# The first down projection of a feed-forward layer: its instruction order written out on all engines

## The chip, the cores and the metric

The kernel runs on one core of one Trainium2 chip. The core has five engines, each with its own stream of instructions: TensorE (PE in the profile; its weight loads are PEld) multiplies 128x128 stationary tiles with 128x512 moving tiles; VectorE (DVE) does elementwise work and reads the accumulators; ScalarE (ACT) copies, squares and scales; GpSimd (POOL) does elementwise work between tiles in the on-chip memory; SyncE (SP) only issues transfers, and its stream is called the load queue here.

The metric is the device time of one execution, in microseconds (us).

## The reference

One layer of a diffusion backbone for 2048 tokens of width 1024 in float32: attention and a gated recurrence, an output projection, and then a gated feed-forward layer. What the change touches is the last part:

```python
def swiglu(h, w_gu, w_down):
    a, b = jnp.split(h @ w_gu, 2, axis=-1)
    return (jax.nn.silu(a) * b) @ w_down
...
        x = x + mx[5] * swiglu(modulate(rmsnorm(x, g_norm2[l]), mx[3], mx[4]), w_gu[l], w_down[l])
...
    return rmsnorm(x, g_final)
```

`w_gu` is 1024 x 5632 and `w_down` 2816 x 1024. The kernel keeps float32 accuracy by splitting each factor into a rounded high part and the rest (two tiles, "parts"), and multiplies high by high, high by low and low by high.

## The kernel before, in words

Attention, recurrence and output projection end at about 2010 us. The feed-forward layer then runs in four stages, and the tokens are handled as two pairs of 512-token blocks, pair 1 first: `hidden(1)`, `down(1)`, `hidden(0)`, `down(0)` (lines 1520 to 1526).

Both matrix products use a seven-product scheme (Strassen and Winograd's) over a 2x2 split: left factors A11, A12, A22 and sums S1 to S4, right factors B11, B21, B22 and sums T1 to T4. So there are seven products of half the size, and their accumulators are partly carried from one product to the next.

**`hidden(pair, side, made)`** (line 1243), the up projection, runs over 22 blocks of 128 columns. For each, `weights` loads two 512 KB pieces of `w_gu` into the pool `wraw` (two tiles of each of two tags), makes parts of A11 and A12, then the sums S1, S2, S4, S3 on GpSimd (`total`, pool `wsum`) and their parts (line 1264 copies on ScalarE, line 1265 subtracts). Line 1291 is its matmul, 12 per product. The results go to memory, with sums of them for the next stage (lines 1355 to 1361, stored at 1306). `made` is a generator that makes the right factors' parts during the first block; `side` is called after every second block. In pair 1 `side` is `right_sums` (line 1368): for each of 11 row blocks of `w_down` it loads four quadrants of 256 KB into the 10-tile pool `tmp`, makes four sums on VectorE (lines 1378 to 1384) and stores them.

**`down(pair, side)`** (line 1388), the down projection, has 7 products of 11 steps, so 77 steps. `load(i)` (lines 1415, 1416) fetches two 256 KB tiles into `wraw`; `exact(i)` makes their parts, two copies on ScalarE (line 1429) and two subtractions on VectorE (line 1430); `mms(i, t)` (line 1484) does 3 matmuls for each of 4 token blocks, 12 in a step. In pair 1 the parts lie in two sets of tiles, `dwa` and `dwb`, for even and odd steps; in pair 0 they lie in the 32 tiles of `vA`. After the last step of a product `emptied` (line 1453) handles one of its four accumulators in each following step: gate product on VectorE (line 1460), addition to the row block on GpSimd (line 1461), for the fourth to sixth product a square on ScalarE (line 1446), for the fifth another product on GpSimd (line 1466), and for the sixth the row's normalization: sum (1450) and mean (119) on VectorE, a power on GpSimd (121), scaling on VectorE (1469) and the store (1470). The last product does the same at the end (1474, 1476, 1477). `side` is called in every sixth step; in pair 1 it is `build(0)` (line 1201), which reloads the other pair's right factors (line 1214) and makes their parts (lines 1112, 1113) and sums (1177, 1206, 1228), several tiles in one call.

**Order.** A planner arranges each engine's stream from the program's order, priorities and its own estimate of times; it may take instructions of one stage ahead of another's. `tc.high_priority()` moves a piece forward. `tc.manual_schedule(engines=...)` marks a region in which the named engines issue the region's instructions in the order of the program's text; where instructions from outside the region fall among them stays the planner's choice. Before, no such region lies in the feed-forward stages.

**Places.** The pools of `hidden` (`wva`, `wsum`, `wvb`) and those of `down` (`y0p`, `dwa`, `dwb`, `y1p`) share memory: `wva` lies where `y0p` lies, `wsum` where `dwa` lies, `wvb` where `dwb` and `y1p` lie. `vA` (32 tiles) and `vB` (24 tiles) hold the right factors' parts.

## Time and profile before

| | |
|---|---|
| median of 3 runs | 3375.32 us (3370.61 to 3377.19) |
| the profiled execution's own time | 3374.67 us |
| its span, first to last instruction | 3372.9 us |
| mean granted TensorE clock | 0.986 of full speed |
| busy share of the span: TensorE, VectorE, ScalarE, GpSimd | 96%, 54%, 47%, 53% |
| `hidden(1)` | about 2012 to 2465 us |
| `down(1)` | about 2465 to 2712 us |
| `hidden(0)` | about 2712 to 3148 us |
| `down(0)` and the end | 3148 to 3373 us |

How to read it: the profile's windows give, for a stretch of time, each engine's busy time and its count of instructions. TensorE's matmuls overlap, so its busy time nearly fills any stretch in which it is fed; a stretch's loss is better seen from its length against the count of its matmuls. The timeline's rows give start, length, engine, line, operation, output <- inputs with shape, count, and in brackets the idle time of the engine before the row and what ended it. Tile names are without their buffer numbers: `dh` and `dl` are the high and low parts of a down step in pair 1, `lr` the loaded tile, `pd1A` an accumulator, `y` a row block, `yg` the gate product, `sq` the square, `s` and `r` results of the up projection, `w` a loaded piece of `w_gu`, `wq` one of `w_down`; `x` stands for several tiles, the factors' parts among them.

### The profile page before, as it was taken

The page shows a single profiled execution, that of the slowest core. Times are in us where ns is not written, and L with a number is a line of the kernel's source. Part 1 is how long each engine was busy: PE and PEld are TensorE (multiplying, and loading weights), DVE is VectorE, ACT ScalarE, POOL GpSimd, SP SyncE. Part 2 cuts the span into 40 slices and gives each one's busy share as a digit, 9 for nine tenths or more (in the row PEclk, how much of TensorE's full clock was granted, in tenths as well). Part 3 has the DMA queues.
Part 4 walks back from the last instruction along what each step waited for, and adds up shares of the span by engine and source line. Part 5 has one row for each costly group of instructions (what it writes and reads, how often), then busy time and mean ns, then how long its engine had stood idle before and what let it go on. Part 6 is the DMA issues. An engine that isn't in the chain of part 4 may idle for free. (4 is left out here: it accounts for less than half of the span.)

```text
span 3372.9 us, 54914 instructions
## 1 busy us (share of the span) xinstructions
PE 3233.4 (96%) x20220; PEld 2682.1 (80%) x20220; DVE 1836.1 (54%) x3270; ACT 1597.1 (47%) x3327; POOL 1781.8 (53%) x1648
## 2 busy tenths in 40 slices
PE   8999999989999999999999999999979989999998
PEld 5998987987778778778787877888868778888887
DVE  6344555226666666666664556444366753333566
ACT  4322222237777777777764224333344443333444
POOL 4322223118788888888743117767631267666222
PEclk9999999989999999999999999999989999999999
DMA  7244565441111112111015343444565533323764
GB/s 240 87 150 128 164 180 159 121 118 38 42 31 51 56 51 77 38 39 58 18 30 181 119 140 120 159 160 162 170 236 185 191 120 107 97 95 109 252 198 162
DMA packets 358622, 408.04 MB, mean 121 GB/s; under 512 B 31856, under 2 KB 249936, under 8 KB 358096
## 3 DMA queue, kind: packets, MB, share of 16 engines
q1 hardware_dynamic: 358352, 404.53, 37.8%
q8 instruction: 159, 2.61, 0.3%
q14 instruction: 111, 0.91, 0.1%
HBM read 274.92 MB, written 129.52 MB: 120 GB/s over the span
## 5 line engine op out<-in xcount | busy, mean ns | idle before, releaser
L930 DVE TENSOR_REDUCE neg<-s 128x1 f32<-128x768 f32 x384 | 366.5, 955 | 217.3 <-PE s L927 215.9
L943 POOL TENSOR_TENSOR pr<-pr,lf 128x768 f32<-128x768 f32 x256 | 370.9, 1472 | 116.2 <-ACT lf L939 116.1
L927 PE MATMUL s<-K,qs 128*128 128x512 f32 (+1 forms) x1536 | 373.2, 366 | 38.5 <-ACT pr L935 37.1
L935 ACT ACTIVATE pr<-s,neg 128x768 f32<-128x768 f32 x384 | 349.5, 910 | 62.6 <-DVE neg L930 36.3
L927 PEld LDWEIGHTS s<-K,qs 128*128 128x128 f32 x1536 | 263.8, 192 | 118.9 <-ACT pr L935 58.8
L951 PE MATMUL pt<-identr,pr 128*128 128x128 f32 x2304 | 331.9, 277 | 16.8 <-ACT pf L957 12.8
L957 ACT ACTIVATE pf<-pt 128x512 f32<-128x512 f32 x448 | 259.6, 604 | 79.8 <-PE pt L951 76.9
L951 PEld LDWEIGHTS pt<-identr,pr 128*128 128x128 f32 x2304 | 263.6, 142 | 32.2 <-ACT pf L957 24.6
L965 PE MATMUL av<-pf,V 128*64 128x256 f32 x2304 | 260.0, 379 | 0.7 <-DVE neg L934 0.4
L1461 POOL TENSOR_TENSOR y<-y,yg 128x512 f32<-128x512 f32 x48 | 75.8, 1595 | 286.1 <-DVE yg L1460 282.3
L965 PEld LDWEIGHTS av<-pf,V 128*64 128x64 f32 x2304 | 161.3, 137 | 74.6 <-DVE Sb L740 0.6
L1430 DVE TENSOR_TENSOR x<-lr,x 128x512 fp32r<-128x512 f32 x154 | 119.8, 813 | 67.6 <-ACT x L1429 64.9
L1430 DVE TENSOR_TENSOR dl<-lr,dh 128x512 fp32r<-128x512 f32 x154 | 119.0, 810 | 66.3 <-ACT dh L1429 66.2
L1429 ACT ACTIVATE dh<-lr 128x512 fp32r<-128x512 f32 x154 | 89.5, 623 | 110.9 <-PE pd1A L1484 53.9
L1429 ACT ACTIVATE x<-lr 128x512 fp32r<-128x512 f32 x154 | 90.6, 626 | 93.7 <-PE pd0A L1484 38.5
L343 PE MATMUL f<-hTh,wh 128*128 128x512 f32 (+1 forms) x320 | 121.6, 380 | 6.7 <-ACT ft L372 6.7
L1291 PE MATMUL pA<-x,A11h 128*128 128x512 f32 x352 | 114.3, 405 | 8.3 <-ACT A11h L1264 6.0
L1484 PE MATMUL pd0A<-x,x 128*128 128x512 f32 x528 | 120.7, 389 | 0.0
L343 PE MATMUL f<-hTh,wl 128*128 128x512 f32 (+1 forms) x320 | 120.0, 375 | 0.0
L343 PE MATMUL f<-hTl,wh 128*128 128x512 f32 (+1 forms) x320 | 119.5, 373 | 0.0
L121 POOL TENSOR_TENSOR rs_qq<-ms_qq,mhalf 128x4 f32<-128x4 f32 x32 | 35.2, 1102 | 155.3 <-DVE ms_qq L119 151.2
L121 POOL TENSOR_TENSOR rs_x<-ms_x,mhalf 128x1 f32<-128x1 f32 x34 | 20.5, 605 | 181.5 <-DVE ms_x L119 181.5
(332 smaller groups left out, 9131.0 us busy)
## 6 DMA issues: line engine op xcount, KB each, us to landing
w<-in_w_gu_dram SPq DMA_DIRECT2D x88, 512.0 KB
wm<-in_w_mod_dram SPq DMA_DIRECT2D x24, 1024.0 KB
lr<-s_wT SPq DMA_DIRECT2D x88, 256.0 KB
lr<-in_w_down_dram SPq DMA_DIRECT2D x66, 256.0 KB
s_q<-sq SPq DMA_DIRECT2D x128, 128.0 KB
qs<-s_q SPq DMA_DIRECT2D x32, 512.0 KB
wq<-in_w_down_dram SPq DMA_DIRECT2D x44, 256.0 KB
s_wT<-wq SPq DMA_DIRECT2D x44, 256.0 KB
```

What stands on the lines that cost most here:

```text
L343: nc.tensor.matmul(pm[:, :n], w[wi][:, k, c0:c0 + P], hT[b][hi][:, k, :], start=(k == 0 and i == 0), stop=(k == KT - 1 and i == 2))
L927: nc.tensor.matmul(s[:, o:o + w], self.qs[:, hh, self.item[2], half, :], self.kv[0][:, k0 + o:k0 + o + w], start=(half == 0), stop=(half = ...
L930: nc.vector.tensor_reduce(neg[:, i:i + 1], s[:, :n], axis=AX.X, op=ALU.min)
L935: nc.scalar.activation(pr[:, k0:k0 + n], s[:, :n], AF.Exp, bias=neg[:, m:m + 1], scale=-1.0, accum_out=self.lf[:, hh, i, :1] if i < NSEG - ...
L943: nc.gpsimd.tensor_tensor(pj, pj, self.lf[:, hh, j, 1:].to_broadcast([P, SW]), op=ALU.mult)
L951: nc.tensor.transpose(pt[:, (2 * i + hh) * P:(2 * i + hh + 1) * P], self.prs[hh][:, (2 * k2 + i) * P:(2 * k2 + i + 1) * P], ident)
L957: nc.scalar.activation(pf, pt, AF.Copy)
L965: nc.tensor.matmul(self.av[i * 64:(i + 1) * 64], self.kv[1][:, 2 * k2 + i, :], self.pf[k2][:, i * 256:(i + 1) * 256], start=(n == 0), stop ...
L1291: nc.tensor.matmul(acc, w[wi][:, k, :], x[xi][k], start=(start and k == 0 and i == 0), stop=(stop and k == KH - 1 and i == 2), skip_group_ ...
L1429: nc.scalar.activation(hi, src, AF.Copy)
L1430: nc.vector.tensor_tensor(lo, src, f32v(hi), op=ALU.subtract)
L1484: nc.tensor.matmul(cur[t], l[:, t * P:(t + 1) * P], r, start=(start and j == 0 and f == 0), stop=(stop and j == NHF - 1 and f == 2), skip_ ...
```

## The change

1. `build` yields after every tile instead of after every group. `by_factor` restores the old grouping where it runs beside `hidden(1)`. In `down(1)` one tile's work is called in every step from step 8 on (it was a group in every sixth step).
2. `down(1)` is a `manual_schedule` region for all five engines, from after its first loads and parts to its end. `down(0)` is left to the planner.
3. `load` runs 4 steps ahead (it was 3), `exact` 2 steps ahead (it was 1), in pair 1 only up to step 35 and 1 from there on. Four loads and two steps' parts are made under high priority.
4. In pair 1 the parts of steps 0 to 7 lie in `vA`, those of steps 8 to 37 in `vB`, and in `dwa` and `dwb` from step 38 on.
5. The row blocks of pair 1 are loaded in steps 1, 3, 5, 7, 12, 14, 16, 18 (they were in 2 to 9). The stores of finished rows come two steps after their scaling.
6. The last product's work on a row block (`last`) is cut in three pieces: gate product, addition and square; sum, mean and power; scaling and store. The first piece of a token block comes ahead of the second of the one before it, and so on.
7. In the first block of `hidden(0)` S1 and S2 are made under high priority, S1's and S2's sums in `tmp` and their parts in `wva`.
8. `right_sums` is called after each of the first 11 blocks of `hidden(1)`.

The instructions are the same in number and kind. The diff, cut:

```diff
+            eng = nc.gpsimd if pair else nc.vector
...
                         nc.sync.dma_start(x, s_h2[tb][:, k, :])
-                    yield
+                        yield
...
+        def by_factor(steps):
+
+            for x in steps:
+                if x:
+                    yield
...
+                    soon = pair == 0 and ff == 0
...
-                        hi, lo = ((wva if n in ("A11", "A12") else wvb).tile([P, H, P], F32R, tag="v", name=f"{n}{x}{nm}")
+                        hi, lo = ((wva if n in ("A11", "A12") or soon and n in ("S1", "S2") else wvb).tile([P, H, P], F32R, tag="v", name=f"{n}{x}{nm}")
...
                     parts("S2", s2, nc.vector)
+                    if soon:
+                        yield out
...
                     nxt = first(order[0])
+                    if pair == 0:
+                        next(nxt[0])
...
                         h = {}
+                    if n < NHF:
                         next(side, 0)
...
-                        hi, lo = (slot(vA) if pair == 0 else
+                        hi, lo = (slot(vA) if pair == 0 or i < 8 else slot(vB) if i < 38 else
...
-                    (nc.vector if last else nc.gpsimd).tensor_tensor(y[:, cs], y[:, cs], x, op=ALU.add)
+                    nc.gpsimd.tensor_tensor(y[:, cs], y[:, cs], x, op=ALU.add)
...
-                        nc.sync.dma_start(out[0, row(0, t), :], y)
...
+                        stores.append((i + 2, tb, t))
+
+                def last(acc, t):
+
+                    y = ys[1, t]
+                    x = t512(f"yg{pair}l{t}")
+                    nc.vector.tensor_tensor(x, acc, gate2[:, :512], op=ALU.mult)
+                    nc.vector.tensor_tensor(y[:, :512], y[:, :512], x, op=ALU.add)
+                    square(1, 0, t)
+                    yield
+                    rs = norm(1, t)
+                    yield
+                    nc.vector.scalar_tensor_tensor(y[:, :512], y[:, :512], rs, gfin[:, :512],
+                                                   op0=ALU.mult, op1=ALU.mult)
+                    nc.scalar.activation(y[:, 512:], y[:, 512:], AF.Copy, scale=rs)
+                    nc.sync.dma_start(out[0, row(1, t), :], y)
+                    yield
...
+                stores = []
                 with tc.high_priority():
-                    for i in range(3):
+                    for i in range(4):
                         load(i)
                     exact(0)
+                    exact(1)
+                made = 2
...
+                written = ExitStack()
+                if pair:
+                    E = mybir.EngineType
+                    written.enter_context(tc.manual_schedule(engines={E.PE, E.DVE, E.Activation, E.Pool, E.SP}))
                 for i, (n, j) in enumerate(steps):
...
-                    load(i + 3)
-                    exact(i + 1)
+                    load(i + 4)
+                    ahead = 2 if pair == 0 or i < 36 else 1
+                    while made <= i + ahead:
+                        exact(made)
+                        made += 1
                     if i == 0:
                         nc.sync.dma_start(gate2, rows_bcast(modrow[0, 5 * D:6 * D]))
-                    if 2 <= i < 10:
-                        rows((i - 2) // 4, (i - 2) % 4)
+                    if i in ROWS[pair]:
+                        rows(*divmod(ROWS[pair].index(i), 4))
...
                     if pending:
                         emptied(*pending.pop(0))
+                    while stores and stores[0][0] <= i:
+                        _, tb, t = stores.pop(0)
+                        nc.sync.dma_start(out[0, row(tb, t), :], ys[tb, t])
...
-                    if i >= 4 and i % 6 == 0:
+                    if i >= 8:
                         next(side, 0)
+                under = []
                 for t in range(4):
                     for i in range(len(steps) - kept, len(steps)):
                         mms(i, t)
-                    emptied(len(plan) - 1, cur[t], t)
-
-        hidden(1, right_sums(), build(1))
+                    under.append(last(cur[t], t))
+                    for g in reversed(under):
+                        next(g, 0)
+                for _ in range(2):
+                    for g in reversed(under):
+                        next(g, 0)
+                written.close()
+
+        ROWS = (2, 3, 4, 5, 6, 7, 8, 9), (1, 3, 5, 7, 12, 14, 16, 18)
+        hidden(1, right_sums(), by_factor(build(1)))
```

More of the change, by code (lines that the diff above doesn't have):

```diff
@@ L1218, in build @@
                         parts(n, raw[r, 0, k], nc.vector, vA, vA)
-                    yield
-                for _ in early_sums():
-                    yield
+                        yield
+                for (r, tb), (r0, tb0), (r1, tb1) in EARLY:
+                    for k in range(KH):
+                        nc.vector.tensor_tensor(raw[r, tb, k], raw[r0, tb0, k], raw[r1, tb1, k], op=ALU.subtract)
+                        yield
             T1 = [raw.pop((0, 0, k)) for k in range(KH)]
             for t in T1:
-                parts("T1", t, nc.gpsimd if pair else nc.vector, vB, vB)
-            yield
+                parts("T1", t, eng, vB, vB)
+                yield
+            yield "T1"
             T2 = T1
@@ L1228, in build @@
                 nc.vector.tensor_tensor(t, raw[1, 1, k], t, op=ALU.subtract)
+                yield
             for t in T2:
                 parts("T2", t, nc.vector, vB, vB)
-            yield
+                yield
+            yield "T2"
             for k in range(KH):
-                parts("B22", raw.pop((1, 1, k)), nc.gpsimd if pair else nc.vector, vB, vB)
-            yield
-            T4 = [diff(raw.pop((1, 0, k)), T2.pop(0)) for k in range(KH)]
+                parts("B22", raw.pop((1, 1, k)), eng, vB, vB)
+                yield
+            yield "B22"
+            T4 = []
+            for k in range(KH):
+                T4.append(diff(raw.pop((1, 0, k)), T2.pop(0)))
+                yield
             for k in range(KH):
                 parts("T3", raw.pop((0, 1, k)), nc.vector, vA, vA)
-            yield
+                yield
+            yield "T3"
             for t in T4:
-                parts("T4", t, nc.gpsimd if pair else nc.vector, vA, vA)
-            yield
+                parts("T4", t, eng, vA, vA)
+                yield
+            yield "T4"
+        def by_factor(steps):
+            for x in steps:
+                if x:
+                    yield
         def hidden(pair, side, made):
@@ L1268, in total @@
                     def total(n, x, y, op):
-                        t = wsum.tile([P, H, P], F32, tag="s", name=f"{n}{nm}")
+                        t = t512(f"{n}{nm}").rearrange("p (h c) -> p h c", c=P) if soon and n in ("S1", "S2") else \
+                            wsum.tile([P, H, P], F32, tag="s", name=f"{n}{nm}")
                         nc.gpsimd.tensor_tensor(t, x, y, op=op)
```

14 lines of the change are left out of this document (5 added, 9 removed).

## The prediction

> **What bounds the kernel now.** I read the windows by stage first, then TensorE's timeline wherever a window is worse than its pace, then the other engines and the load queue (SP) at those places. The two feed-forward halves are limited by TensorE: from 2760 to 3148 us, and in the second pair's down projection after that, it never idles. The first pair's down projection (about 2465 to 2712) is the exception, and the change rewrites it. The first fence holds windows (length; busy time and count of each engine; clock; DMA share; GB/s), then the matmuls of line 1484 alone, then one TensorE row.
>
> ```profile
> 2451.00:2520.00 69.00, 52.17 (x200) 40.16 (x198) 48.56 (x71) 29.53 (x52) 23.02 (x9) 0.85 0.66 226
> 2520.00:2600.00 80.00, 77.64 (x340) 63.61 (x341) 48.95 (x67) 32.31 (x56) 13.42 (x9) 1.00 0.59 189
> 2600.00:2660.00 60.00, 55.89 (x242) 44.84 (x241) 44.67 (x55) 30.70 (x60) 17.72 (x12) 1.00 0.52 170
> 2660.00:2713.00 53.00, 50.47 (x209) 39.53 (x207) 34.02 (x53) 22.13 (x42) 10.27 (x9) 0.97 0.63 208
> 2713.00:2760.00 47.00, 39.27 (x153) 31.12 (x154) 28.93 (x40) 22.39 (x43) 32.21 (x26) 0.89 0.32 101
> 2760.00:3148.00 388.00, 388.00 (x1658) 311.93 (x1657) 138.06 (x160) 141.11 (x237) 260.70 (x195) 1.00 0.34 111
> ```
>
> ```profile
> 2451.00:2713.00 262.00, 221.69 (x924) 176.58 (x924) 0.95 0.60 198
> 3148.00:3364.00 216.00, 209.89 (x924) 173.43 (x924) 1.00 0.61 205
> ```
>
> ```profile
> 3359.82 4.24 PE L1484 MATMUL pd0A<-x,x 128*128 128x512 f32 x18
> ```
>
> The same 924 matmuls take 262 us here and 216 there (some matmuls of a neighbouring stage lie in each window). Eighteen in a row take 4.24 us, and the last is 0.39 us long, so the pace is (4.24 - 0.39) / 17 = 0.2265 us; a step of 12 is 2.72 us. In the up projection it is 388 / 1658 = 0.234 us. Length minus count times pace gives what each stretch loses: 69 - 45.3 = 23.7; 80 - 77.0 = 3.0; 60 - 54.8 = 5.2; 53 - 47.3 = 5.7; and 47 - 153 x 0.234 = 11.2 at the start of the next up projection. That is 48.8 us, all a change here can win.
>
> The start, in rows of a timeline (start, length, engine, line, what; in brackets the idle time before it and what ended it):
>
> ```profile
> 2476.23 0.79 PE L1484 MATMUL pd1A<-dl,dh 128*128 128x512 f32 x1 [1.54 <-DVE dl L1430]
> 2476.82 0.63 PE L1484 MATMUL pd1A<-dh,dl 128*128 128x512 f32 x1
> ...
> 2495.35 0.80 PE L1484 MATMUL pd1A<-dl,dh 128*128 128x512 f32 x1 [8.88 <-DVE dl L1430]
> ```
>
> ```profile
> 2472.70 12.47 POOL L1361 TENSOR_TENSOR s<-r,s 128x512 f32<-128x512 f32 x1 [6.10 <-DVE r L1348]
> 2485.20 0.33 SPq L1306 DMA_DIRECT2D s_hid1S<-s  x1
> 2491.26 0.63 ACT L1429 ACTIVATE dh<-lr 128x512 fp32r<-128x512 f32 x1 [5.87 <-DMA lr<-s_hid1A]
> ```
>
> The 8.88 us gap is a chain: VectorE is full of the other pair's factors, one GpSimd subtraction takes 12.47 us, its store heads the load queue until 2485.20, with the next step's load behind it, and ScalarE waits 5.87 us for that load. After gaps of 1.5 and 8.9 us the next matmuls are 0.63 us long instead of 0.39, so a gap costs some 1.5 us more.
>
> **The change part by part.** *Start of the stage.* Steps 0 to 7 put their parts in tiles of the old factors, two steps are prepared and four loaded under high priority, the other pair's factors come one tile per step from step 8 on, and the w_down sums are over by then. Every item of the chain above is gone. What is late next is one accumulator bank that waits for the last product of the old stage; nine matmuls (2 us) cover it. I leave 1.0 of the 23.7: **-22.7** (bounds -16.3, if stores still head the queue for the 5.87 us of the ScalarE row and the clock falls, and -23.7). DMA: a step needs 0.5 MB, from step 8 to 23 another 0.26 MB of factors, and between 12 and 18 also half a row block, so 1.05 MB in 2.72 us, 385 GB/s. This row gives 40 slices of the time from 2440 to 2712, and shows 401 reached:
>
> ```profile
> GB/s 380 401 342 236 352 89 71 290 283 170 222 89 237 217 173 217 96 235 200 182 143 216 180 219 176 170 192 232 171 198 128 134 137 175 224 177 220 325 254 112
> ```
>
> With four loads ahead I count nothing for it; without the lead, each GB/s short is a later load.
>
> *Two steps ahead up to step 35.* The 3.0 us of 2520 to 2600 are the emptied banks of the first products, where four additions on GpSimd (5.95 us) stretch four subtractions on VectorE to 5.46. A step ahead covers this: **-3.0** (bounds 0 and -3.0).
>
> ```profile
> 2515.58 5.95 POOL L1461 TENSOR_TENSOR y<-y,yg 128x512 f32<-128x512 f32 x4 [30.41 <-DVE yg L1460]
> 2517.21 5.46 DVE L1430 TENSOR_TENSOR dl<-lr,dh 128x512 fp32r<-128x512 f32 x4
> ```
>
> *The written order from step 36 on.* Here only one step is prepared ahead, in two sets of tiles, and the text puts the emptying of a bank between one step's parts and the next: gate product (VectorE), addition (GpSimd), square (ScalarE), for the sixth product also sum, mean, power and scaling of the row. In written order the square stands before the next step's copies on ScalarE. In the profile the planner did it the other way:
>
> ```profile
> 2637.35 1.29 DVE L1430 TENSOR_TENSOR dl<-lr,dh 128x512 fp32r<-128x512 f32 x2 [1.43 <-ACT dh L1429]
> 2638.56 0.68 DVE L1460 TENSOR_TENSOR yg<-pd1A,gate 128x512 f32<-128x512 f32 x1
> 2639.32 1.30 POOL L1461 TENSOR_TENSOR y<-y,yg 128x512 f32<-128x512 f32 x1 [19.40 <-DVE yg L1460]
> 2639.40 1.15 ACT L1429 ACTIVATE dh<-lr 128x512 fp32r<-128x512 f32 x2 [1.56 <-PE pd1A L1484]
> 2640.66 0.63 ACT L1446 ACTIVATE sq<-y 128x512 f32<-128x512 f32 x1
> ```
>
> ```profile
> 2617.37 0.63 ACT L1446 ACTIVATE sq<-y 128x512 f32<-128x512 f32 x1 [1.53 <-POOL y L1461]
> 2618.00 1.13 ACT L1429 ACTIVATE dh<-lr 128x512 fp32r<-128x512 f32 x2
> 2618.65 2.42 DVE L1430 TENSOR_TENSOR dl<-lr,dh 128x512 fp32r<-128x512 f32 x2 [0.16 <-ACT dh L1429]
> ```
>
> The copies (2639.40) ran while GpSimd added, the square after them (2640.66). In the new order one round is: copy to subtraction 0.65 (2618.00 to 2618.65), two subtractions 1.21 (2637.35 to 2638.56), gate product until the addition starts 0.76, addition 1.30 and 0.04 to the square, square until the next copy 0.63: 4.6 us against 2.72. Four banks are emptied: the last subtraction is done 4 x 4.6 + 0.65 + 1.29 = 20.3 us after the first copy, and TensorE, unhindered, would want it at 5 x 2.72 + 0.23 = 13.8. That is 6.5, and 1.5 for the slow matmuls behind the gap: **+8.0** for the fourth product. For the fifth, three of the four rounds also hold a copy (0.53) and a subtraction (0.60, half the pair's) of a factor: 3 x 5.7, and 5.1 for the last, whose subtractions meet the extra GpSimd product: 22.2 + 1.94 - 13.8 = 10.3, with the clock **+11.8**. For the sixth, VectorE itself waits in the middle:
>
> ```profile
> 2716.92 0.19 ACT L1446 ACTIVATION_READ_ACCUMULATOR sq<-y 128x1 f32 x1
> 2717.14 0.16 DVE L1450 TENSOR_TENSOR ss1f<-ssf 128x1 f32<-128x1 f32 x1 [0.19 <-ACT sq L1446]
> 2717.82 0.15 DVE L119 TENSOR_SCALAR ms_xf<-ss1f 128x1 f32<-128x1 f32 x1
> 2718.05 0.55 POOL L121 TENSOR_TENSOR rs_xf<-ms_xf,mhalf 128x1 f32<-128x1 f32 x1 [2.85 <-DVE ms_xf L119]
> 2690.57 1.28 DVE L1469 SCALAR_TENSOR_TENSOR y<-y,rs_xf,gfin 128x1024 f32<-128x1024 f32 x1 [0.38 <-POOL rs_xf L121]
> 2691.77 0.68 DVE L1430 TENSOR_TENSOR dl<-lr,dh 128x512 fp32r<-128x512 f32 x1
> ```
>
> From a copy to the square 3.96, square and its sum 0.73, then 0.03, sum 0.18, mean to power 0.23, power 0.55, 0.03, scaling 1.20 (2690.57 to 2691.77): 6.9. Subtraction to subtraction that is 6.9 - 0.65 = 6.26, and 6.86 in the three rounds that also hold a factor: 26.8 + 1.94 - 13.8 = 14.9, with the clock **+16.6**. The sum of the three is +36.4. The 5.2 + 5.7 lost there now fall away: **-10.9**. Bounds of the pair of terms: +15 (no slow matmuls, each round 0.5 us shorter) to +34 (each round 0.7 longer).
>
> The Trainium skill, Perfetto Trace Analysis, "Tensor Engine Instruction", calls ScalarE, VectorE and GpSimd strict first-in first-out, which is the rule that speaks against this part: what waits at the head holds all behind it. The trace agrees: the copy at 2618.00 starts as the square ends, and the square had waited 1.53 us.
>
> *Start of the next up projection.* S1 and S2 of its first block are made ahead, with places of their own. Now:
>
> ```profile
> 2728.15 1.22 PE L1291 MATMUL pA<-x,A11h 128*128 128x512 f32 x2 [6.01 <-ACT A11h L1264]
> 2729.14 0.61 ACT L1264 ACTIVATE S1h<-S 128x512 fp32r<-128x512 f32 x1
> 2697.28 11.07 SPq L1256 DMA_DIRECT2D w<-in_w_gu_dram  x4
> 2722.26 0.36 SPq L1477 DMA_DIRECT2D out_dram<-y  x1
> 2704.79 0.64 ACT L1264 ACTIVATE A11h<-w 128x512 fp32r<-128x512 f32 x1 [2.89 <-DMA w<-in_w_gu_dram]
> ```
>
> TensorE waits 6.01 us with the next block's product, and S1's copy runs only at 2729.14; had it been there, four products of 12 (11.2 us) would cover the rest. The first bank is free in time too: the gate product comes first in the new last piece. I leave 2 of 11.2: **-9.2** (bounds 0 and -11.2).
>
> *First sums moved.* The w_down sums run beside the first 11 blocks of the first up projection instead of every second one: the same 44 loads, 44 sums, 44 stores, now also at its start, where VectorE is busy 18.51 of 20 us:
>
> ```profile
> 2040.00:2060.00 20.00, 17.03 (x73) 13.08 (x71) 18.51 (x19) 13.00 (x24) 14.98 (x10) 0.99 0.00 1
> ```
>
> Four sums more are 4 x 0.60 = 2.4 us there. They are emitted behind the block's own work, so I take **+1.5** (bounds -1 and +6; the upper one is four loads short of a tile, waiting 1.5 us each). *Last tiles.* In the second pair the last square comes ahead of a scaled copy that waits: **-1**. Loads and two steps ahead in that pair: 0, as TensorE never idles there.
>
> Sum: -22.7 - 3.0 + 36.4 - 10.9 - 9.2 + 1.5 - 1 = **-8.9 us**. The profiled execution took 3374.67, 0.65 below the median; 3374.67 - 8.9 = 3365.8, so 3366. From no change a measurement tells 0.2%, 6.7 us, on either side.
>
> **The rivals.** (1) *Slower: the next weights queue behind the last stores.* Their loads are outside the written part. Should SP hold them behind the stores of the last finished rows, which wait for their scaling, they go out when the first store did, at 2722.26, 9 us after the down projection's end at 2713, and land 7.5 us later (2697.28 to 2704.79, the time until the first could be copied). TensorE then idles 16.5 us and has slow matmuls for 1.5 behind that, not 2 in all: +16.0 on the sum, 3382. From 15.6 us of added loss on (8.9 + 6.7) the change is slower by what can be told. For: a store at the head held the loads until 2485.20. Against: the four went out at 2697.28, well before the stores. (2) *The emptying is covered* after all, as the planner's order covered it (2.4 us of stretched subtractions, no TensorE gap at 2617): no +36, time 3330, and between this and the sum for half of it, 3348. Against: two sets of tiles and the order of the text. (3) *The first sums collide*: the ten other blocks each lose 1 to 2 us to a load that waits for one of the pool's 10 tiles (ten of 1 in place of the 1.5: 3374, of 2: 3384). Against: with a set in every second block TensorE was busy for 369.41 of 371 us there, by the window:
>
> ```profile
> 2080.00:2451.00 371.00, 369.41 (x1578) 296.66 (x1577) 160.45 (x190) 133.22 (x226) 256.26 (x187) 1.00 0.51 168
> ```
>
> (4) *No slow matmuls behind short gaps.* In this kernel that would take 1.5 from each of the three terms: 3361. The Trainium skill, TensorE: Matmul & The Clock Gate, "What's actually happening", has the clock fall only after an idle window of about 3.4 us. The trace does not bear that out here: the matmul at 2476.82 is 0.63 us long after a gap of 1.54.
>
> **How the numbers follow.** Forecast 0.48 (its own range 3357 to 3374), rival 1 0.18, rival 2 0.14, rival 3 0.12, rival 4 0.05, unnamed 0.03. Faster: 0.28 of the forecast, 0.14 of rival 2, 0.05 of rival 4: 0.47. Same: 0.20 of the forecast, 0.07 of rival 3, 0.03 of rival 1: 0.30. Slower: 0.15 of rival 1, 0.05 of rival 3 and the unnamed: 0.23. The range 3344 to 3388 leaves out the better half of rival 2 and the far end of rival 1.
>
> **What would show it.** Right: no gap over 2 us from the down projection's first matmul until the fourth product's banks are emptied; then three groups of four gaps, about 2, 3 and 4 us, each ended by the subtraction, with ScalarE's square waiting for GpSimd ahead of the copies, and VectorE's mean and scaling ahead of subtractions; S1's copy before the last down matmul. Wrong: a stage near 216 us (rival 2), a gap over 6 us ended by a w_gu load (rival 1), or gaps between 2100 and 2300 us (rival 3).

## The result and the profile after

The changed kernel took **3387.71 us** (median of 8 runs, 3381.48 to 3398.99), the kernel before, run beside it, 3372.49 us (8 runs, 3367.30 to 3377.19). The ratio is 1.0047, with a 95% interval of 1.0031 to 1.0063: slower by 0.47%, where 8.9 us, 0.26%, faster was forecast. The time lies within the range that the prediction gave (3344 to 3388), but at its far end and on the other side of no change. The profiled execution took 3384.43 us, its span is 3382.7 us, the clock 0.988.

The first views show where to look: up to TensorE's first up-projection matmul the program is unchanged, so time is counted from there.

```profile
L1291 PE MATMUL pA<-x,A11h x2: 394/396/397, 2011.9 to 2012.2; 128*128 128x512 f32 x2
```

```profile
L1317 PE MATMUL pA<-x,A11h x8: 392/397/400, 2006.0 to 2010.3; 128*128 128x512 f32 x8
```

The first row is of the kernel before, the second of the changed one: that line's TensorE instructions with their first and last start. To the span's end it is 3372.9 - 2011.9 = 1361.0 us before and 3382.7 - 2006.0 = 1376.7 after, **+15.7 us**. That is the medians' difference, 15.2; the spans differ by only 9.8 because this execution happened to come to the up projection 5.9 us sooner. It was 6.0 us ahead already at the last matmul of line 705 (1725.0 us against 1731.0), long before anything that the change touches.

The windows of the changed kernel (columns as in the prediction: length; busy time and count of TensorE, its weight loads, VectorE, ScalarE, GpSimd; clock; DMA share; GB/s):

```profile
2085.00:2461.00 376.00, 366.10 (x1545) 292.37 (x1544) 170.86 (x192) 132.57 (x227) 252.48 (x184) 0.99 0.50 163
2461.00:2510.00 49.00, 44.69 (x188) 35.99 (x187) 23.88 (x29) 18.05 (x30) 9.80 (x6) 0.97 0.67 236
2510.00:2595.00 85.00, 85.00 (x377) 70.35 (x376) 64.10 (x89) 38.23 (x66) 16.78 (x10) 1.00 0.67 229
2595.00:2633.00 38.00, 33.91 (x135) 25.70 (x134) 22.26 (x37) 17.63 (x35) 5.81 (x4) 0.96 0.48 153
2633.00:2674.00 41.00, 33.75 (x134) 25.66 (x134) 25.28 (x37) 18.14 (x36) 10.24 (x8) 0.96 0.43 141
2674.00:2713.00 39.00, 28.39 (x96) 20.88 (x95) 21.84 (x38) 14.15 (x29) 7.33 (x8) 0.82 0.49 162
2713.00:2760.00 47.00, 41.45 (x164) 31.95 (x163) 33.93 (x41) 22.57 (x44) 31.64 (x23) 0.93 0.36 119
```

With the prediction's paces (0.2265 us for a down matmul, 0.234 for an up matmul), length minus count times pace gives each stretch's loss:

| stretch | before | after | difference | predicted |
|---|---|---|---|---|
| first sums (2085 to 2461) | 1.7 | 14.5 | **+12.8** | +1.5 |
| start of `down(1)` (2461 to 2510) | 23.7 | 6.4 | **-17.3** | -22.7 |
| two steps ahead (2510 to 2595) | 3.0 | 0 | -3.0 | -3.0 |
| emptying of the 4th, 5th, 6th product (2595 to 2713) | 10.9 | 7.4 + 10.6 + 17.3 = 35.3 | +24.4 | +36.4 - 10.9 = +25.5 |
| start of `hidden(0)` (2713 to 2760) | 11.2 | 8.6 | **-2.6** | -9.2 |
| last tiles | 8.8 | 8.8 | 0 | -1 |
| sum | | | +14.3 | -8.9 |

The last row is the time from the end of the last matmul to the span's end. The 1.4 us between 14.3 and 15.7 lie outside these windows or in their edges.

*The first sums.* TensorE and ScalarE, then VectorE, then the load queue, all of the changed kernel. Line 1404 loads a quadrant of `w_down`, lines 1407 to 1413 are its sums, 1365 and 1358 a sum of the up projection and the copy that follows it, 1332 a store of its results:

```profile
2097.05 0.73 PE L1317 MATMUL pB<-x,S4h 128*128 128x512 f32 x2 [3.11 <-ACT r L1358]
2096.41 0.60 ACT L1358 ACTIVATE r<-pB 128x512 f32<-128x512 f32 x1 [5.59 <-DVE r L1365]
```

```profile
2088.33 0.69 DVE L1407 TENSOR_TENSOR wq<-wq,wq 128x512 f32<-128x512 f32 x1 [3.59 <-DMA wq<-in_w_down_dram]
...
2094.44 0.68 DVE L1407 TENSOR_TENSOR wq<-wq,wq 128x512 f32<-128x512 f32 x1
2095.04 0.68 DVE L1365 TENSOR_TENSOR r<-pB,r 128x512 f32<-128x512 f32 x1
```

```profile
2084.22 0.32 SPq L1332 DMA_DIRECT2D s_hid1S<-s  x1
2084.59 1.87 SPq L1404 DMA_DIRECT2D wq<-in_w_down_dram  x4
```

VectorE stands 3.59 us at a `w_down` sum whose load went out at 2084.59, behind a store. Five sums, the last of them of the next set, come ahead of the up projection's own sum at 2095.04; ScalarE's copy (line 1358) follows it, and TensorE has idled 3.11 us. Four more gaps of over 0.2 us follow, of 2.64, 2.04, 0.50 and 1.46 us, the last at 2258.85. Up to 2260 us all eleven sets of sums have begun (line 1407, from 2053.8 to 2256.2); in the kernel before it was five (line 1378, from 2093.6 to 2240.5).

*The emptying.* ScalarE and VectorE around the sixth product's rounds:

```profile
2685.20 0.63 ACT L1475 ACTIVATE sq<-y 128x512 f32<-128x512 f32 x1 [4.57 <-POOL y L1489]
...
2685.83 1.13 ACT L1458 ACTIVATE dh<-lr 128x512 fp32r<-128x512 f32 x2
```

```profile
2675.05 1.29 DVE L1459 TENSOR_TENSOR dl<-lr,dh 128x512 fp32r<-128x512 f32 x2 [0.82 <-ACT dh L1458]
...
2681.91 1.29 DVE L1459 TENSOR_TENSOR dl<-lr,dh 128x512 fp32r<-128x512 f32 x2
...
2688.17 1.29 DVE L1459 TENSOR_TENSOR dl<-lr,dh 128x512 fp32r<-128x512 f32 x2
```

The step's copies (2685.83) stand behind a square that waited 4.57 us for GpSimd. From subtraction to subtraction it is 6.86 and 6.26 us, the two values that the prediction gave for a round with and without a factor's tile.

*The start of `hidden(0)`.* TensorE, ScalarE and GpSimd:

```profile
2732.80 1.22 PE L1317 MATMUL pB<-x,S1h 128*128 128x512 f32 x2 [3.07 <-ACT S1h L1287]
```

```profile
2732.13 0.62 ACT L1287 ACTIVATE S1h<-S 128x512 fp32r<-128x512 f32 x1
```

```profile
2727.64 0.92 POOL L121 TENSOR_TENSOR rs_xf<-ms_xf,mhalf 128x1 f32<-128x1 f32 x1 [1.03 <-DVE ms_xf L119]
2728.54 1.29 POOL L1294 TENSOR_TENSOR S<-w 128x512 f32<-128x512 f32 x1
```

S1's sum was not made ahead. It runs at 2728.54, after the second of the last rows' powers, which are in the written part, and its copy comes after the last down matmul (2726.54).

### The profile page after: what moved, and what is told of

It reads as the page before. It is cut to its first block, busy times and chain, and to the rows that moved or that the text cites. A ratio compares the mean times of both kernels' runs of the same rounds, so it can differ in the third digit from the quotient of the medians.

```text
span 3382.7 us, 54886 instructions
## 1 busy us (share of the span) xinstructions
PE 3238.4 (96%) x20220; PEld 2681.5 (79%) x20220; DVE 1846.6 (55%) x3270; ACT 1594.8 (47%) x3327; POOL 1771.1 (52%) x1648
## 5 line engine op out<-in xcount | busy, mean ns | idle before, releaser
L1459 DVE TENSOR_TENSOR x<-lr,x 128x512 fp32r<-128x512 f32 x230 | 184.7, 841 | 83.5 <-ACT x L1458 78.3
L1458 ACT ACTIVATE x<-lr 128x512 fp32r<-128x512 f32 x230 | 136.4, 626 | 147.4 <-PE pd0A L1521 38.5
L1317 PE MATMUL pB<-x,S4h 128*128 128x512 f32 x352 | 112.5, 400 | 5.8 <-ACT r L1358 5.8
L1317 PE MATMUL pA<-x,A22h 128*128 128x512 f32 x352 | 112.8, 402 | 5.3 <-DVE r L1369 5.3
L1317 PE MATMUL pB<-x,S1h 128*128 128x512 f32 x352 | 113.3, 401 | 3.1 <-ACT S1h L1287 3.1
```

What stands on the lines that cost most here:

```text
L1317: nc.tensor.matmul(acc, w[wi][:, k, :], x[xi][k], start=(start and k == 0 and i == 0), stop=(stop and k == KH - 1 and i == 2), skip_group_ ...
L1458: nc.scalar.activation(hi, src, AF.Copy)
L1459: nc.vector.tensor_tensor(lo, src, f32v(hi), op=ALU.subtract)
```

## The experiments

Times are medians; each ratio is to the kernel before, run on the same chip, with its 95% interval. "To the end" is the time from the first up-projection matmul to the span's end in the profiled execution, as above (1361.0 before, 1376.7 for the changed kernel). It comes from one execution of each kernel, and executions differ: e3's ten lie between 3348.99 and 3367.77 us, the profiled one took 3355.58; e5's eight lie between 3377.24 and 3394.04, the profiled one took 3379.31.

| kernel | median us | ratio | to the end |
|---|---|---|---|
| e1_sums_back | 3372.29 | 0.9992 (0.9978 to 1.0006) | 1365.4 |
| e2_sums_only | 3383.33 | 1.0024 (1.0008 to 1.0040) | 1374.5 |
| e3_square_later | 3363.08 | 0.9962 (0.9945 to 0.9978) | 1349.7 |
| e4_planner | 3357.91 | 0.9955 (0.9940 to 0.9970) | 1349.1 |
| e5_s12_vector | 3390.16 | 1.0040 (1.0019 to 1.0061) | 1372.9 |
| e6_places | 3385.74 | 1.0047 (1.0034 to 1.0061) | 1372.5 |
| e7_all | 3350.06 | 0.9937 (0.9916 to 0.9958) | 1334.9 |
| e8_split | 3387.11 | 1.0047 (1.0028 to 1.0065) | 1376.9 |
| e9_planner_all | 3338.60 | 0.9922 (0.9899 to 0.9944) | 1331.5 |
| e10_own_places | 3397.57 | 1.0083 (1.0066 to 1.0099) | 1387.2 |
| e11_all_own | 3359.28 | 0.9973 (0.9962 to 0.9983) | 1351.8 |
| e12_sums_mid | 3373.19 | 1.0001 (0.9985 to 1.0018) | 1363.6 |

### The first sums: one part undone, one part alone

e1 takes the changed kernel and puts the call back into every second block; e2 takes the kernel before and makes only this move:

```diff
 e1, on the changed kernel
-                    if n < NHF:
                         next(side, 0)
 e2, on the kernel before
                         h = {}
+                    if n < NHF:
                         next(side, 0)
```

> The changed kernel with one part undone: the w_down sums run beside every second block of the first up projection again. Theory A (each moved part costs or gains in its own stage, by what stands ahead of a wait in an engine's stream): the gaps between 2090 and 2465 us, 9.9 us idle and 14.6 us lost in the changed kernel, fall back to about 2 us, and the rest stays as it is, so about 13 us less than the changed kernel, ratio to the kernel before 1.001. Rival B (the first sums are not the cause; the planner only shifted other work there): loss of that stretch stays above 10 us, ratio 1.004 to 1.005.

> The kernel before with one part done alone: the w_down sums run beside each of the first 11 blocks. Theory A: the stretch from 2090 to 2465 us loses about 13 us more than before; the start of the down projection gains what the last set of sums took there, at most some 5 us; ratio 1.002 to 1.004. Rival B: no change in that stretch, ratio 1.000.

The window of the up projection in e1, then in e2:

```profile
2086.00:2447.00 361.00, 358.79 (x1525) 288.11 (x1524) 156.91 (x188) 131.11 (x222) 243.45 (x179) 1.00 0.49 161
```

```profile
2090.00:2464.00 374.00, 364.51 (x1539) 290.92 (x1538) 163.72 (x186) 130.45 (x222) 251.34 (x184) 0.99 0.51 165
```

361 - 1525 x 0.234 = 4.2 us lost with the move undone (1.7 in the kernel before), 374 - 1539 x 0.234 = 13.9 with the move alone. To the end, e1 is 11.3 us under the changed kernel and e2 13.5 over the kernel before. The place of the term is shown from both sides, and the move alone brings 12.2 of its 12.8 us. The size also depends on what the planner makes of it: with the same text of this stage, e3 below loses 11.3 us in this stretch (367 us, 1520 matmuls) and e4 18.6 (374 us, 1519 matmuls).

### The first sums: what makes them cost

The chain above has two candidates ahead of VectorE's wait: the loads go out late, behind the stores (e8 issues a set's loads one block ahead of its sums), or they wait for one of the pool's ten tiles (e10 gives them four tiles of their own).

```diff
 e8
-                    if n < NHF:
+                    if n <= NHF:
                         next(side, 0)
...
                         nc.sync.dma_start(t, quadrant(r, c, j))
+                yield
...
                 nc.sync.dma_start(s_wt["T4"][j], b[1, 0])
-                yield
 e10
+                if pair:
+                    sums_at.append(pool(d1, "wqp", 4))
...
-                        t = b[r, c] = tmp.tile([P, 512], F32, tag="x", name=f"wq{j}{r}{c}")
+                        t = b[r, c] = sums_at[0].tile([P, 512], F32, tag="x", name=f"wq{j}{r}{c}")
```

> The changed kernel, with the w_down sums still beside the first blocks, but a set's loads issued one block ahead of its sums. Theory A (the sums stand in VectorE's stream and wait for their loads, with the block's own results behind them): the gaps between 2090 and 2465 us fall from 9.9 us idle to under 4. Rival F (the places of the 10-tile pool or the amount loaded in that stretch sets it): they stay over 8 us or grow, since four tiles are held for a block longer.

> The changed kernel, with one thing added: the w_down pieces of the first sums get four tiles of their own, in memory that is free in that stage, in place of four of the 10 shared with the blocks' results. Theory F (the loads are issued late, since they wait for tiles that the block's results hold, and VectorE's stream then waits for them ahead of the block's own results): the gaps of 2 to 3 us between 2090 and 2265 us go, 9 us and more of the 12 to 15 lost there come back; ratio to the kernel before 1.001 to 1.003. Theory A in its first form (the sums stand in VectorE's stream and wait for their loads, wherever the tiles come from): most of the gaps stay, ratio 1.004 and more.

Neither cured it. In e8 TensorE's gaps there still add up to 7.0 us (9.8 in the changed kernel), between the two expectations; the stretch loses 12.8 us (376 us, 1552 matmuls), and the time to the end is the same. The planner still issued the four loads together and late: its load queue and VectorE show

```profile
2086.33 0.32 SPq L1332 DMA_DIRECT2D s_hid1S<-s  x1
2086.70 1.86 SPq L1404 DMA_DIRECT2D wq<-in_w_down_dram  x4
```

```profile
2091.09 0.79 DVE L1407 TENSOR_TENSOR wq<-wq,wq 128x512 f32<-128x512 f32 x1 [5.93 <-DMA wq<-in_w_down_dram]
```

so moving the text of the loads did not move them, and whether earlier loads would help stays untested. With places of their own, e10, the kernel was slower than the changed one by 10.5 us to the end: the sums were taken still earlier (the first at 2012.42, not 2053.83), two gaps near the start grew from 3.02 and 2.19 us to 6.37 and 3.85 (at 2026.32 and 2059.30), and from 2088 on it lost 17.3 us (387 us, 1580 matmuls), no less than the changed kernel's 14.5. A shortage of tiles is not the cause; that theory fell.

What e10 pointed to is the time, not the tiles, and e12 tests that: the same eleven sets, one per block, six blocks later.

```diff
-                    if n < NHF:
+                    if 6 <= n < 6 + NHF:
                         next(side, 0)
```

> The changed kernel with one edit: the eleven sets of w_down sums are called behind blocks 6 to 16 of the first up projection, one each block, in place of blocks 0 to 10. The density is the same, the start of the stage is left free. The changed kernel loses 14.6 us over the 0.23 us pace between 2090 and 2465 us, in gaps behind VectorE's sums at 2097, 2137, 2142, 2178 and 2259 us that grow smaller with time. Theory H (the sets collide with what the start of the stage leaves behind: x's differences and the first blocks' late weight parts): the stretch loses 2 to 5 us, so the time is 10 to 12 us under the changed kernel's, ratio to before 0.998 to 1.002. Rival J (a set in every block is too dense for VectorE and the load queue wherever it stands): the gaps come back from about 2150 to 2260 us, three to five of 1.5 to 3 us, the loss stays 10 to 15 us, ratio 1.003 to 1.006.

The window of e12, and a row of VectorE in a later block:

```profile
2088.00:2450.00 362.00, 362.00 (x1545) 290.74 (x1545) 170.65 (x195) 131.41 (x222) 251.99 (x182) 1.00 0.54 174
```

```profile
2236.26 0.69 DVE L1407 TENSOR_TENSOR wq<-wq,wq 128x512 f32<-128x512 f32 x1 [3.98 <-DMA wq<-in_w_down_dram]
```

The loss is 362 - 1545 x 0.234 = 0.5 us, and the median is 14.5 us under the changed kernel's (13.1 to the end): a little more than the theory of the crowded start asked for, and far from its rival, the dense cadence. VectorE waits as long for such a load as at 2088.33 (3.98 us against 3.59), but TensorE does not idle behind it. So the sums cost because they run beside the first blocks, not because there is one set in each block. What at the start takes away the slack was not separated.

### The emptying: waits placed later, or no written order

e3 keeps the written order but cuts `emptied` into pieces, as the change itself does for the last product: gate product and addition in one step, the square (and the product with `gfin`) in the next, then the mean and power, then the scaling; a row's store comes one step after that and no longer two. e4 takes away only the region, so the planner orders the stage again.

```diff
 e3
+                    if pair:
+                        yield
                     if n == 3 or n == 5:
                         square(0, cb, t)
...
                     if n == 5:
+                        if pair:
+                            yield
                         rs = norm(0, t)
+                        if pair:
+                            yield
...
-                        emptied(*pending.pop(0))
+                        open_.append(emptied(*pending.pop(0)))
+                    for g in list(open_):
+                        if next(g, 1):
+                            open_.remove(g)
 e4
-                if pair:
+                if False:
                     E = mybir.EngineType
```

> The changed kernel, with the same instructions in another written order: in the first down projection the square of an emptied bank comes one step later, behind the next step's copies; the row's sum, mean and power one step after that, its scaling one more. Theory A (the square and the scaling stand ahead of the next step's parts in ScalarE's and VectorE's streams): of the 36 us lost in the three groups of four gaps (fourth, fifth and sixth product) 4 to 8 are left, so ratio to the kernel before 0.995 to 0.997. Rival C (GpSimd's additions slow VectorE's subtractions, or two sets of tiles are too few, wherever the square stands): over 20 of the 36 us stay, ratio over 1.000.

> The changed kernel without the written region: places, loads, steps ahead, first sums and the sums S1 and S2 stay as changed, the planner orders all engines. Theory A: the planner puts the squares behind the copies, so the three groups of gaps shrink from 36 to some 5 to 12 us, and the start of the stage is worse than 6 us again, since the other pair's factors come early; ratio 0.996 to 1.002. Rival C: the three groups stay above 20 us, as they do not come from the order; ratio 1.003 and more.

The windows of the three products in e3, then in e4:

```profile
2591.00:2623.00 32.00, 30.90 (x134) 24.64 (x133) 25.45 (x35) 17.88 (x35) 5.83 (x4) 1.00 0.56 181
2623.00:2656.00 33.00, 30.73 (x132) 24.13 (x132) 28.48 (x36) 18.27 (x36) 12.68 (x8) 1.00 0.53 176
2656.00:2698.00 42.00, 35.79 (x139) 27.73 (x138) 33.35 (x52) 19.30 (x39) 10.32 (x9) 0.92 0.58 188
```

```profile
2594.00:2624.00 30.00, 30.00 (x133) 24.47 (x132) 20.18 (x26) 15.26 (x30) 5.97 (x4) 1.00 0.60 193
2624.00:2661.00 37.00, 32.91 (x135) 25.89 (x134) 28.50 (x36) 17.63 (x34) 12.61 (x9) 0.95 0.48 157
2661.00:2697.00 36.00, 34.17 (x147) 26.98 (x147) 26.00 (x40) 15.26 (x31) 9.46 (x8) 1.00 0.66 219
```

e3 loses 1.6 + 3.1 + 10.5 = 15.2 us, more than the 4 to 8 expected but under its rival's 20, and e4 -0.1 + 6.4 + 2.7 = 9.0, against 35.3 in the changed kernel. So most of this loss comes from the written order, and both kernels end 27 to 28 us earlier; the three products are not all of that. In e3 they bring 20.1 us, the start of `hidden(0)` 3.7 (4.9 lost, 47 us from 2698 with 180 matmuls) and the first sums 3.2. In e4 they bring 26.3, and the start of `down(1)`, which was expected to be worse than 6 us again, loses 0.2 (50 us, 220 matmuls) and so brings 6.2; the first sums and the start of `hidden(0)` (10.5 lost, 47 us from 2697 with 156 matmuls) take 6.0 back. The squares wait less in e3 (1.72 us for GpSimd at 2635.39, where the same square of the changed kernel waits 3.52), since their addition went out a step before, and TensorE's gaps in this product shrink with that: the longest is 1.00 us, against 1.49. Part of what e3 still loses is a new wait: one of its copies stands behind a copy of the next stage's weights that waits for its load, and TensorE idles 3.53 us behind that.

```profile
2689.24 0.63 ACT L1287 ACTIVATE A11h<-w 128x512 fp32r<-128x512 f32 x1 [2.56 <-DMA w<-in_w_gu_dram]
2689.77 0.61 ACT L1458 ACTIVATE dh<-lr 128x512 fp32r<-128x512 f32 x1
```

### The start of `hidden(0)`

e5 gives the sums of S1 and S2, and S1's low part, to VectorE, to get them out of GpSimd's stream:

```diff
-                        nc.gpsimd.tensor_tensor(t, x, y, op=op)
+                        (nc.vector if soon and n in ("S1", "S2") else nc.gpsimd).tensor_tensor(t, x, y, op=op)
...
-                    parts("S1", s1, nc.gpsimd)
+                    parts("S1", s1, nc.vector if soon else nc.gpsimd)
```

> The changed kernel, with S1 and S2 of the next up projection's first block, and S1's low part, made on VectorE in place of GpSimd. Theory A (they came late because the planner put GpSimd's S1 behind the powers of the last rows, which wait for the written tail): S1's copy comes before the down projection's end, the 3.07 and 1.04 us gaps go, the start of the next up projection loses 2 to 4 us in place of 9.2. Rival D (S1 is late because the weights land late, whatever makes the sum): both gaps stay within 1 us of their size.

VectorE, then TensorE, in e5:

```profile
2724.78 0.15 DVE L119 TENSOR_SCALAR ms_xf<-ss1f 128x1 f32<-128x1 f32 x1
2724.85 0.68 DVE L1294 TENSOR_TENSOR S<-w 128x512 f32<-128x512 f32 x1
```

```profile
2727.72 1.08 PE L1317 MATMUL pB<-x,S1h 128*128 128x512 f32 x2 [2.80 <-ACT S1h L1287]
```

The gap before S1 stays at 2.80 us (3.07 in the changed kernel), which is the size that the rival of late weights asked for. But the four loads of weights have gone out by 2715.9, no transfer runs from 2719 to 2722, and S1's sum starts at 2724.85, so the weights lay ready. GpSimd's stream was not what held the sum either: on VectorE, too, it stands behind most of the written last rows' work. Why the planner puts a high-priority piece there was not shown. The gap goes with the order of the emptying: before S1's matmul TensorE idles 0.68 us in e3 and 0.64 in e7 below, which cut it into pieces, and 5.98 in e4 and 5.68 in e9, which have no region; how the one leads to the other is not shown.

### The start of `down(1)`

The 6.4 us left there hold two gaps, of 1.11 and 3.20 us. VectorE's stream in the changed kernel and the larger gap:

```profile
2471.52 4.18 DVE L1459 TENSOR_TENSOR x<-lr,x 128x512 fp32r<-128x512 f32 x3 [0.90 <-ACT x L1458]
2475.62 0.68 DVE L1376 TENSOR_TENSOR r<-pA,r 128x512 f32<-128x512 f32 x1
```

```profile
2476.35 7.81 PE L1521 MATMUL pd1A<-x,x 128*128 128x512 f32 x26 [3.20 <-DVE r L1376]
```

Three of the new stage's subtractions stand ahead of the old stage's last product (line 1376), whose accumulator TensorE needs. Steps 4 to 7 take tiles of `vA`, which the last up-projection matmuls still read. e6 puts those four steps in `vB`:

```diff
-                        hi, lo = (slot(vA) if pair == 0 or i < 8 else slot(vB) if i < 38 else
+                        hi, lo = (slot(vA) if pair == 0 or i < 4 else slot(vB) if i < 38 else
```

> The changed kernel, with the parts of steps 4 to 7 in places of vB, which the old stage leaves earlier than the places of vA. Theory A (two of the old stage's results stood on VectorE behind subtractions that waited for a place of vA): the gaps of 1.11 and 3.20 us at the start of the down projection go and that start loses 1 us in place of 6.4. Rival E (VectorE's own load, with GpSimd beside it, makes the results late): the 3.20 us gap stays over 2 us.

```profile
2465.00:2510.00 45.00, 43.43 (x190) 35.13 (x189) 17.89 (x26) 14.23 (x25) 8.52 (x6) 1.00 0.74 257
```

45 - 190 x 0.2265 = 2.0 us are left of 6.4, and both gaps are 0.78 us. The median does not resolve 4 us of 3386; to the end e6 is 4.2 us under the changed kernel.

### Together

e7 puts e1, e3, e5 and e6 together; e11 is e7 with e10's places in place of e1's edit; e9 is e7 without the written region and without e3's pieces (so e1, e4, e5 and e6).

> The changed kernel with four things mended: first sums at their old place, the square and the scaling later in the written order, parts of steps 4 to 7 in vB, S1 and S2 on VectorE. Theory A: the gains add, as each lies in its own stretch: 13 + 22 + 5 + 5 us below the changed kernel, so 3340 to 3346 us, ratio to the kernel before 0.988 to 0.992. A rival that has them share one cause (VectorE's load) would give less than 30 us together, ratio over 0.994.

> The first sums beside the first 11 blocks as in the changed kernel, but with places of their own; square and scaling later in the written order; parts of steps 4 to 7 in vB; S1 and S2 on VectorE. If F holds, this is at least as fast as the kernel with the sums at their old place (3342.98 us in its profiled run, ratio 0.9937): 0.990 to 0.994. If not, it is some 10 us slower than that, ratio 0.996 to 0.998.

> As the kernel with all four mended, but the planner orders the first down projection: no written region, the square where the planner puts it. Theory A: the planner's order costs no more than the mended written order, as the loss came from the place of the square and the scaling, not from who chose the order: within 6 us of it, ratio 0.992 to 0.996. Rival G (a written order is worth something by itself, once it is right): over 8 us slower than it, ratio above 0.996.

The stage in e9, from its start through the three emptied products:

```profile
2443.00:2491.00 48.00, 48.00 (x211) 39.40 (x210) 33.45 (x50) 20.37 (x37) 14.73 (x10) 1.00 1.00 370
...
2577.00:2607.00 30.00, 30.00 (x134) 24.73 (x133) 20.16 (x26) 15.41 (x31) 5.27 (x5) 1.00 0.59 194
2607.00:2644.00 37.00, 32.90 (x132) 25.83 (x131) 28.33 (x35) 17.34 (x34) 12.16 (x8) 0.91 0.47 156
2644.00:2681.00 37.00, 34.87 (x149) 27.11 (x148) 26.21 (x40) 15.48 (x31) 9.51 (x8) 1.00 0.65 213
```

e7 is 41.8 us under the changed kernel to the end, e9 45.2, and e9 is the fastest kernel of the study: 3338.60 us, 0.78% under the kernel before (0.56% to 1.01%). Its stage starts without a loss (48 - 211 x 0.2265 = 0.2) and loses -0.3 + 7.1 + 3.3 = 10.1 in the three products. What it keeps of the change (the places, two steps ahead, the other pair's factors tile by tile, the last product in pieces) carries the gain; these were not separated. The written order adds nothing that can be measured: the intervals of e7 and e9 overlap. e11 lies 16.9 us above e7 to the end: places of their own do not replace e1's edit.

## Why the prediction was wrong, step by step

*First sums moved* is the step that failed. It priced one set more, four sums of 0.60 us, at the busy start and took +1.5, with +6 as the upper end; it measured +12.8. The change puts six sets more ahead of 2260 us, not one, and the prediction's ground, "emitted behind the block's own work", does not hold in the planned stream: five sums stood ahead of line 1365. Rival 3 had the right place and nearly the size (ten blocks of 1 to 2 us), but its mechanism, a load waiting for one of ten tiles in every block, is not it: e10 rejects the tiles, e12 the cadence, and there were five gaps, the last at 2258.85. With +12.8 in the place of +1.5 the prediction's sum is +2.4, no change.

*Start of the stage* was mis-sized: -17.3 against -22.7, near the end that the prediction took from stores at the head of the queue, but for another reason. What is late next was named rightly, the accumulator that waits for the last product of the old stage; that nine matmuls would cover it was wrong, because the new stage's subtractions stand ahead of that product on VectorE. e6 shows it.

*Start of the next up projection* failed as well: -2.6 against -9.2. "S1 and S2 are made ahead" was read off the change's text, and the planner did not do it. These three explain the direction: (12.8 - 1.5) + (22.7 - 17.3) + (9.2 - 2.6) = 23.3, of the 24.6 between -8.9 and +15.7.

*The written order* was right: 35.3 against 36.4, and 7.4, 10.6 and 17.3 against 8.0, 11.8 and 16.6 (a slip: 14.9 and 1.5 make 16.4). The rounds of the sixth product came out to 0.02 us. Within the fourth, two misses cancel. Three of its rounds are 4.96 us and not 4.6. They hold a factor's sum on VectorE (line 1235) that the prediction did not count there, and beside it GpSimd's addition starts later (1.12 us after the gate product, not 0.76) or takes longer (1.61 us at 2608.07, not 1.30); the first round, without such a sum, is 4.65:

```profile
2602.29 0.68 DVE L1488 TENSOR_TENSOR yg<-pd1B,gate 128x512 f32<-128x512 f32 x1
...
2607.25 0.69 DVE L1488 TENSOR_TENSOR yg<-pd1B,gate 128x512 f32<-128x512 f32 x1
```

```profile
2603.41 1.32 POOL L1489 TENSOR_TENSOR y<-y,yg 128x512 f32<-128x512 f32 x1 [3.64 <-DVE yg L1488]
```

The other miss is the 1.5 us charged for slow matmuls. They came, seven of 0.63 us from 2613.48 on (the last section shows the first), but behind them TensorE still waits for a subtraction, at 2617.28, so by these rows they fill time in which it would have idled. The fifth product has the same: eight from 2647.13 on, and a wait for a subtraction at 2652.96. So rival 4, no slow matmuls, did not happen, though its saving came in two of the three groups. The row that the prediction held against it shows less than it was taken for: in the kernel before, the matmuls ahead of the gap of 1.54 us were already 0.63 us long (from 2473.22 on), behind a gap of 4.46 us at 2469.59.

*Two steps ahead* was right (-3.0 both). *Last tiles* were worth 0, not -1. Rival 1 did not happen: no gap over 6 us ended by a load of `w_gu`. Rival 2 did not happen in the changed kernel; e3 and e4 show what it would have been worth.

## What to carry to other kernels

Price a written order by its rounds: add up every wait that the text puts ahead of the next step's work on each engine, and cut a chain that crosses three engines into pieces, one per step, so that what a piece waits for was issued a step before. Check against the written order what the planner makes of the same work: in the three products it lost less here (9.0 us against 15.2 for the order in pieces). Work that a planner still places, inside or beside a written region, need not be where the text puts it, nor where a priority asks for it: give it a range of the whole slack it may eat, and look for the stretch of the stage that has none. Moving side work to the beginning of a stage can cost nearly as much as the work lasts, even on an engine that is far from full (12.8 us for six sets of four sums of 0.60, 14.4 us in all, on a VectorE that is busy for 171 of 376 us), and six blocks later nothing.

## What the runs showed of the hardware

Slow matmuls need no long gap, and they need not start behind one. In the changed kernel's fourth product a gap of 1.36 us is followed by matmuls of 0.39 us, and the seven of 0.63 start two microseconds later, with no gap but one of 0.30 us between. In its sixth a gap of 2.07 is followed by matmuls of 0.39 and 0.40, and one of 1.99 by eleven of 0.63 from 2690.10 on:

```profile
2611.53 0.50 PE L1521 MATMUL pd1A<-dh,dh 128*128 128x512 f32 x1 [1.36 <-ACT dh L1458]
...
2613.48 0.63 PE L1521 MATMUL pd1A<-dh,dl 128*128 128x512 f32 x1
...
2617.28 0.50 PE L1521 MATMUL pd1A<-dl,dh 128*128 128x512 f32 x1 [0.24 <-DVE dl L1459]
```

```profile
2683.26 0.50 PE L1521 MATMUL pd1A<-dl,dh 128*128 128x512 f32 x1 [2.07 <-DVE dl L1459]
2683.59 0.39 PE L1521 MATMUL pd1A<-dh,dl 128*128 128x512 f32 x1
...
2689.51 0.80 PE L1521 MATMUL pd1A<-dl,dh 128*128 128x512 f32 x1 [1.99 <-DVE dl L1459]
```

The same gaps can also end differently. In the fifth product e4 and e9 both have a gap of 0.77 us, four matmuls, and a gap of 2.90 and 2.91; in e9 the next matmuls take 0.63 us at once (2626.86), in e4 0.39 and 0.40, and 0.63 only from 2645.52 on, 1.6 us after the gap's end. The granted clock was 0.96 in the fourth and fifth product's windows of the changed kernel and 0.82 in the sixth's. The Trainium skill, TensorE: Matmul & The Clock Gate, "What's actually happening", has the clock fall only after an idle window of about 3.4 us; the changed kernel's three products do not agree with that by a single gap, as none is over 2.07 us and each has slow matmuls, and how much idle time in several gaps it takes, no run here separates.

The time to the first up-projection matmul, whose part of the program no kernel here changes, was between 2004.1 and 2014.7 us in the fourteen profiled executions, each of another kernel. The range is two thirds of the effect measured here, so one span against one span would have misjudged it; the time from that matmul to the end agrees with the medians.
